# Seven pairs of 128-column blocks of an input projection, half of their rows by products of 2x2 blocks; weight sums moved from VectorE to GpSimd

## The chip, the cores and the metric

The kernel runs on one core of a Trainium2 chip. The metric is the device time of one execution in microseconds (us), as the median of three runs. Engines are named as in the profile: PE (TensorE, its weight loads apart as PEld), DVE (VectorE), ACT (ScalarE), POOL (GpSimd), SP (SyncE, here only an issuer of DMAs).

## The reference

One layer of a decoder: a norm, one input projection, three kinds of token mixers on disjoint heads, one output projection, a last norm. There are 512 tokens behind 16 meta tokens, 2048 channels, and all of it is float32.

```python
h = rms_norm(concat(meta, x), norm_w)              # 528 rows of 2048
proj = h @ w_in                                    # 2048 x 7585 columns
# 6 DeltaNet heads:  dq, dk, dv -> causal conv, SiLU, chunked delta rule, norm, * silu(dz)
# 5 GLA heads:       gq, gk, gv -> gated linear attention, norm, * silu(gz)
# 5 attention heads: logits = (fq * 128**-0.5) @ fk.T + c_t - c_s, causal softmax,
#                    o_fox = probs @ fv * silu(fz)
o = concat(o_dn, o_gla, o_fox)                     # 16 heads of 128
y = rms_norm(x + o @ w_out, final_norm_w)
```

## The kernel before

It is one program. A scheduler sets the order of the instructions on each engine from the order in the program, priorities and waits; pools of a fixed number of buffers set when a tile can be used again. There is a place where the order is written out by hand: `PLACE`, `PM` and `behind` put some matmuls of the mixers behind a given matmul of the projection, so that TensorE has projection work while other engines prepare a mixer's step.

**Arithmetic.** A float32 product is made of three passes of TensorE over operands that are split exactly into two parts, high and low: high by high, high by low, low by high. The norm's weight is worked into the transposed input when it is loaded, and its 16 tiles of 128 channels (k-tiles) stay in SBUF as `xh` and `xl`, 528 columns each. A weight tile is loaded by SP into `raw` (128x1024), its high part is made by ScalarE (L150), its low part by VectorE (L151), at the highest priority (`split`). The pool `wp` holds two each of `raw`, `hi` and `lo`.

**Input projection.** `inproj(key)` makes a block of 128 output columns for all tokens: two weight tiles of 8 k-tiles, each k-tile with three passes (`inproj_part`, L207). With the meta tokens a pass is two matmuls of 264 columns, which go to two PSUM banks; without them it is one of 512. The pool `psb` has four such banks, `psm` four more for all else. `evac` (L325) then multiplies with 1/rms of each token (`rstd`) on VectorE.

**Order of the work.** Four dz blocks while x is loaded; the gates; DeltaNet in two groups of three heads, each `dn_keys`, `dn_values`, `dn_queries`, `dn_inverse`, `dn_mix`; the gz gates; GLA in three pairs of heads; five attention heads; the output projection; the norm. `conv_silu` makes DeltaNet's keys, values and queries: `evac`, four VectorE instructions of convolution (L418), then `silu`, whose first step is on GpSimd (L334), three on ScalarE and the last on VectorE (L338). Behind it TensorE transposes keys (L490, tile `pk`) and values (L628, tile `pv`).

**Attention.** `fox_head(h)` makes the blocks fk and fv (with meta tokens), fq and fz (without), and then four blocks of 128 queries with softmax. The gated output stays in a tile of the pool `zp` (or a `gd` or `six` tile).

**Output projection.** The heads are ordered 6 DeltaNet, 5 GLA, 5 attention. The last eight go through plain products (`mms`, L1068). The first eight (`SH`) are taken in pairs of heads, as 2x2 blocks, by seven products in place of eight (Winograd's form). This needs sums of weight blocks: `weight_sums(j, half)` loads four 128x512 blocks of `w_dn`, makes four subtractions on VectorE (L432) in a tile of `six` and stores them to DRAM (`tw`). Eight calls of it stand in attention heads 0 to 3 (`SUMS`). The sums of the operands begin in `first_sums` (VectorE, attention head 4). The final weight is applied by GpSimd (L1092).

The output's accumulators and the gated heads share `zp`, 11 tiles of 128x512.

## Time and profile before

| | |
|---|---|
| median of three runs | 1009.97 us (1009.96, 1009.97, 1011.5) |
| the profiled execution | 1010.53 us |
| its span in the trace | 1008.8 us |
| granted TensorE clock, mean | 0.998 |
| moved by DMA | 128.13 MB, mean 127 GB/s |
| idle time of TensorE in the span | 1008.8 - 995.7 = 13.1 us |

The span reaches from the first to the last instruction in the trace; the run takes 1.7 us more. The profile gives busy times of each engine, the chain of waits that ended last, groups of instructions by line and tile with the wait before them, and the engines' pieces in time. A row of a group reads: line, engine, operation, output and inputs with their shape, count; busy time and mean duration; idle time just before, and what ended it.

### The profile page before, as it was taken

How to read it: one execution, taken by the hardware profiler on the slowest of the kernel's cores; microseconds unless marked ns; L12 is line 12 of the kernel's file. 1: busy time of each engine (PE TensorE's matmuls, PEld its weight loads, DVE VectorE, ACT ScalarE, POOL GpSimd, SP SyncE). 2: the span in 40 equal slices, each digit the busy share in tenths (PEclk: the TensorE clock that was granted, in tenths of full speed). 3: DMA queues.
4: the chain of work that ended last, by engine and by line, in shares of the span. 5: the costliest groups of instructions: out<-in, count | busy, mean ns of one | idle time of the engine just before them, and what ended most of it. 6: DMA issues, size and time to landing. Idle time of an engine off the chain costs nothing.

```text
span 1008.8 us, 19003 instructions
## 1 busy us (share of the span) xinstructions
PE 995.7 (99%) x7614; PEld 898.7 (89%) x7614; DVE 618.2 (61%) x1342; ACT 433.1 (43%) x948; POOL 138.6 (14%) x141
## 2 busy tenths in 40 slices
PE   9999999999999999999999999999999999999996
PEld 7899999899999888898989988889898988888885
DVE  6366767865566985244646474655363747677673
ACT  7654533434456334244445444342323244354354
POOL 0021411211112322101111010100101010000060
PEclk9999999999999999999999999999999999999999
DMA  9623233233222223231221272543362635466634
GB/s 351 229 67 119 82 93 96 102 101 104 75 86 75 94 90 101 68 94 59 84 64 50 66 244 82 189 138 93 120 226 95 237 119 188 127 193 226 181 109 167
DMA packets 53357, 128.13 MB, mean 127 GB/s; under 512 B 11949, under 2 KB 15197, under 8 KB 53268
## 3 DMA queue, kind: packets, MB, share of 16 engines
q1 hardware_dynamic: 39008, 115.30, 34.5%
q10 hardware_dynamic: 14260, 11.61, 4.1%
q8 instruction: 60, 0.98, 0.4%
q14 instruction: 29, 0.24, 0.1%
HBM read 113.32 MB, written 13.44 MB: 126 GB/s over the span
## 4 chain that ended last, share of the span: by engine, by line
PE 92%; DVE 3%; ACT 1%; DMA 1%; POOL 1%; issue 1%; ACTq 1%; SPq 0%; DVEq 0%; POOLq 0%
PE pp L207 57%; PE pa L1068 5%; PE pq L1068 4%; PE pp L261 4%; PE pt L1068 4%; PE ps L1068 2%; PE pss L822 1%; PE pr L1068 1%; POOL stgz L334 1%; PE pgate L361 1%; PE pfo L990 1%; PE pfa L957 1%; DVE wlo L151 1%; DVE ot L556 1%; PE pg L523 1%
## 5 line engine op out<-in xcount | busy, mean ns | idle before, releaser
L207 PE MATMUL pp<-xl,whi 128*128 128x264 f32 (+2 forms) x1456 | 378.1, 310 | 0.0
L207 PE MATMUL pp<-xh,whi 128*128 128x264 f32 (+2 forms) x1456 | 376.3, 310 | 0.8 <-DVE fqk L325 0.7
L207 PE MATMUL pp<-xh,wlo 128*128 128x264 f32 (+2 forms) x1456 | 375.4, 309 | 0.4 <-DVE wlo L151 0.4
L207 PEld LDWEIGHTS pp<-xh,whi 128*128 128x128 f32 x1456 | 243.1, 188 | 15.1 <-issue 1.4
L207 PEld LDWEIGHTS pp<-xl,whi 128*128 128x128 f32 x1456 | 244.3, 189 | 13.6 <-issue 0.2
L207 PEld LDWEIGHTS pp<-xh,wlo 128*128 128x128 f32 x1456 | 243.7, 188 | 14.1 <-DVE wlo L151 0.8
L150 ACT CAST whi<-raw 128x1024 fp32r<-128x1024 f32 x110 | 115.3, 1048 | 184.7 <-PE pp L207 158.1
L151 DVE TENSOR_TENSOR wlo<-raw,whi 128x1024 fp32r<-128x1024 f32 x110 | 134.4, 1222 | 88.8 <-ACT whi L150 78.2
L334 POOL TENSOR_SCALAR stc<-cv 128x528 f32<-128x528 f32 (+1 forms) x18 | 28.2, 1566 | 138.2 <-DVE cv L418 115.2
L418 DVE SCALAR_TENSOR_TENSOR cv<-pb,cpk,cv 128x528 f32<-128x528 f32 (+1 forms) x54 | 40.7, 755 | 0.7
L1068 PE MATMUL pa<-whio,ol 128*128 128x512 f32 x72 | 28.5, 396 | 0.0
L1068 PE MATMUL pa<-wloo,oh 128*128 128x512 f32 x72 | 28.3, 393 | 0.0
L325 DVE TENSOR_TENSOR pb<-pp,rstd 128x264 f32<-128x264 f32 (+1 forms) x36 | 13.7, 423 | 23.3 <-PE pp L207 23.3
L432 DVE TENSOR_TENSOR ws<-ws 128x512 f32<-128x512 f32 x32 | 21.6, 686 | 9.7 <-DMA ws<-in_w_dn 9.6
L150 ACT CAST whis<-raws 128x1024 fp32r<-128x1024 f32 x16 | 16.8, 1051 | 24.8 <-PE pq L1068 9.7
L151 DVE TENSOR_TENSOR wlos<-raws,whis 128x1024 fp32r<-128x1024 f32 x16 | 19.5, 1222 | 12.7 <-ACT whis L150 12.7
L1068 PE MATMUL pa<-whio,oh 128*128 128x512 f32 x72 | 26.6, 399 | 0.0
L977 ACT CAST fphi<-pfx 128x384 fp32r<-128x384 f32 (+2 forms) x20 | 8.0, 399 | 41.0 <-PE pfx L974 38.2
L966 ACT ACTIVATE fp<-fp,fsm 128x144 f32<-128x144 f32 (+3 forms) x20 | 11.5, 574 | 29.8 <-DVE fsm L965 29.7
L150 ACT CAST whio<-rawo 128x1024 fp32r<-128x1024 f32 x13 | 13.7, 1051 | 24.1 <-PE pa L1068 12.8
L334 POOL TENSOR_SCALAR stfz<-zfz 128x512 f32<-128x512 f32 x5 | 10.6, 2126 | 94.9 <-ACT whi L150 47.8
L1092 POOL TENSOR_TENSOR acc<-acc,fw 128x512 f32<-128x512 f32 x3 | 4.6, 1564 | 135.2 <-ACT sqf L1089 135.2
(439 smaller groups left out, 1642.7 us busy)
## 6 DMA issues: line engine op xcount, KB each, us to landing
raw<-in_w_in SPq DMA_DIRECT2D x110, 512.0 KB, 3.3
ws<-in_w_dn SPq DMA_DIRECT2D x32, 256.0 KB, 4.7
tw<-ws SPq DMA_DIRECT2D x32, 256.0 KB, 3.5
rawo<-in_w_out SPq DMA_DIRECT2D x13, 512.0 KB, 3.4
raws<-tw SPq DMA_DIRECT2D x12, 512.0 KB, 4.6
xt<-in_xtok SPq DMA_DIRECT2D x8, 512.0 KB, 8.7
rawa<-in_w_dn SPq DMA_DIRECT2D x8, 512.0 KB, 3.6
xs<-in_xT SPq DMA_DIRECT2D x7, 528.0 KB, 7.1
```

Of the source, the lines that this page charges most:

```text
L150: pace[0] = A.copy(hi, raw).ins
L151: pace[1] = V.tensor_tensor(out=lo, in0=raw, in1=hi.bitcast(F32), op=ALU.subtract).ins
L207: mm = PE.matmul(p_[:, :nt], wt[:, j * m : (j + 1) * m], xx[k][:, t0 : t0 + nt], start=(k == 0 and wt is hi and xx is xh), stop=(k == KT - ...
L261: mm = PE.matmul(ps[:, :S], wt[:, j * P : (j + 1) * P], xx[k][:, NM:T], start=(k == 0 and wt is hi and xx is xh), stop=(k == KT - 1 and wt ...
L325: V.tensor_tensor(out=o, in0=p_[rows], in1=rstd[rows, t0 : t0 + n], op=ALU.mult)
L334: G.tensor_scalar_max(t, src, LOW)
L361: PE.matmul(pgate[a][:, :HT], wg[k // 8][:, k % 8, :], xx[k][:, a * HT : (a + 1) * HT], start=(k == 0 and xx is xh), stop=(k == KT - 1 and ...
L418: V.scalar_tensor_tensor(out=c, in0=pb[:, t0 + w : w + T], scalar=cwc[:, blk, w : w + 1], in1=c, op0=ALU.mult, op1=ALU.add)
L432: sub = lambda o, a, b: V.tensor_tensor(out=o, in0=a, in1=b, op=ALU.subtract)
L523: PE.matmul(pg[:r, j * r : (j + 1) * r], kT[:, j, ts], kT[:, j, ts], start=True, stop=True)
L966: A.activation(pr[:, : m + P], pr[:, : m + P], AF.Exp, bias=sm[:, 2:3], accum_out=sm[:, 3:4])
L1068: PE.matmul(p_, o_[:, s], w_, start=(first and n == 0), stop=(last and n == 2), skip_group_check=True)
```

## The change

Three things change together.

**Pairs of blocks.** In attention heads 1 to 4 the four blocks are taken as two pairs, (fk, fq) and (fv, fz); the first of them, (fk, fq) of head 1, is left as it was, so seven pairs remain. `inproj_pair` makes both blocks of a pair. Of the 16 k-tiles, 0 to 3 and 8 to 11 form a product of 2x2 blocks: two blocks of columns by two halves of channels, times two halves of channels by two halves of tokens (264 each, `lo_` with the meta tokens and `hi_`). It is made as seven products of blocks; the other eight k-tiles are added plainly. All of it runs in four PSUM banks (a, b, c, d), in 15 calls of `mm` with 12 matmuls each. Four blocks of summed weights come from DRAM (`ti`), made ahead by `in_sums` on GpSimd. The sums of x are made by `x_sums` (GpSimd, with splits on ScalarE and VectorE), and the last by `x_last`, which overwrites the second half of `xh` and `xl` of k-tiles 0 to 3 in head 1.

**Weight sums.** `weight_sums` runs on GpSimd too, with its staging in `zp` in place of `six`. Its eight calls and the seven of `in_sums` stand between the steps of DeltaNet (`AHEAD`): in the first group behind `dn_keys` three `in_sums`, behind `dn_values` three, behind `dn_queries` one, behind `dn_inverse` two `weight_sums`; the other six in the second group.

**Room.** Gated DeltaNet heads and the first two GLA heads are stored to DRAM (`zd`) and loaded again ahead of the output projection, so that their tiles are free for staging and for `x_sums`. `zp` has 12 tiles of 128x528. `first_sums` runs on GpSimd, as a step of the output projection.

```diff
+NK = 4
+H1 = 1
+SKIP = 1
+LATE = 1
+ZK = 3
...
-    zp = pool("zp", 11)
+    zp = pool("zp", 12)
...
+    def in_sums(n):
+        h, one, two = PAIRS[n]
+        x, y, z = stage(f"is{n}")
+        get = lambda o, key, half: nc.sync.dma_start(out=o, in_=w_in[BLOCK_OF[key, h], half][:, :KC])
+        put = lambda i, t: nc.sync.dma_start(out=ti[n][:, i], in_=t)
+        two_ = lambda o, a, b, op: G.tensor_tensor(out=o, in0=a, in1=b, op=op)
+        get(x, two, 0)
+        get(y, two, 1)
+        get(z, one, 0)
+        two_(y, x, y, ALU.add)
+        two_(x, z, x, ALU.subtract)
+        put(0, y)
+        two_(z, y, z, ALU.subtract)
+        put(2, x)
+        put(1, z)
+        get(x, one, 1)
+        two_(x, x, z, ALU.subtract)
+        put(3, x)
...
+    def x_sums(ks):
+        for k in ks:
...
+            two = lambda o, p_, q_, op=ALU.subtract: G.tensor_tensor(out=o, in0=p_, in1=q_, op=op)
+            two(a, B(0, 0, 1), B(0, 0, 0))
+            two(b, B(1, 0, 1), B(1, 0, 0))
+            two(a, a, b, ALU.add)
+            parts("t1", 0, a)
+            two(b, B(0, 1, 1), a)
+            two(b, b, B(1, 1, 1), ALU.add)
+            parts("t2", 1, b)
+            two(a, B(0, 1, 0), b)
+            two(a, a, B(1, 1, 0), ALU.add)
+            parts("t4", 2, a)
...
+    def x_last(last):
...
+            else:
+                A.copy(xh[k][:, HT:], xr[k])
+                V.tensor_tensor(out=xl[k][:, HT:], in0=xr[k], in1=f(xh[k]), op=ALU.subtract)
+
+    def inproj_pair(n, c1, c2, tmp):
...
+        w1, w2 = tile_of("1", both(b1, head_))
+        mm(a, w1, xs_(up, lo_), True, True)
+        A.copy(ta, a[:, :HT])
+        mm(b, w2, xs_(dn, lo_), True)
+        def two():
...
+            w1, w2 = tile_of("2", ti[n][:, 0:2])
+            mm(d, w1, sums("t1"), True, True)
+            A.copy(tb, d[:, :HT])
+            mm(a, w2, sums("t2"), False, True)
+            V.tensor_tensor(out=tb, in0=a[:, :HT], in1=tb, op=ALU.add)
+
+        def three():
...
+            w1, w2 = tile_of("3", both(b1, rest_))
+            mm(b, w1, xs_(r0, lo_))
+            mm(b, w2, xs_(r1, lo_), False, True)
+            V.tensor_tensor(out=c1[:, lo_], in0=b[:, :HT], in1=ta, op=ALU.add)
+            mm(c, w1, xs_(r0, hi_), True)
+            mm(c, w2, xs_(r1, hi_))
+
+        c = d = None
+        for f in (three, two) if n < LATE else (two, three):
+            f()
+        w1, w2 = tile_of("4", ti[n][:, 2:4])
+        mm(a, w1, xs_(up, hi_), False, True)
+        A.copy(ta, a[:, :HT])
+        mm(c, w2, xs_(dn, hi_), False, True)
+        V.tensor_tensor(out=c1[:, hi_], in0=c[:, :HT], in1=tb, op=ALU.add)
+        w1, w2 = tile_of("5", w_in[b2, 0][:, rest_], w_in[b2, 1][:, head_])
+        mm(d, w1, xs_(r0, hi_))
+        mm(a, w2, sums("t4"), cols=dead)
+        mm(a, w1, xs_(r0, lo_), cols=dead)
+        w1, = tile_of("6", w_in[b2, 1][:, rest_])
+        mm(d, w1, xs_(r1, hi_), False, True)
+        V.tensor_tensor(out=c2[:, hi_], in0=d[:, :HT], in1=ta, op=ALU.add)
+        mm(a, w1, xs_(r1, lo_), False, True, cols=dead)
+        A.copy(c2[:, dead], a[:, dead])
...
-        w = six.tile([P, 3, 512], F32, tag="six", name=f"ws{j}{half}")
-        x, y, z = (w[:, i] for i in range(3))
+        x, y, z = stage(f"ws{j}{half}")
...
-        sub = lambda o, a, b: V.tensor_tensor(out=o, in0=a, in1=b, op=ALU.subtract)
+        sub = lambda o, a, b: G.tensor_tensor(out=o, in0=a, in1=b, op=ALU.subtract)
...
+            if 2 * p + e < SH - DN_HEADS:
+                nc.sync.dma_start(out=zd[DN_HEADS + 2 * p + e], in_=o)
...
+            n = 2 * (h - H1) - SKIP
...
+                inproj_pair(n, kT, qT, qk[:, 1])
+                G.tensor_tensor(out=kT, in0=kT, in1=rstd, op=ALU.mult)
...
+            if h == H1:
+                x_last(True)
...
+            inproj_pair(n + 1, v, zr, qk[:, 1])
+            G.tensor_tensor(out=v, in0=v, in1=rstd, op=ALU.mult)
+            vhi, vlo, v3, vm = values(v)
+            G.tensor_tensor(out=zr[:, NM:], in0=zr[:, NM:], in1=rstd[:, NM:], op=ALU.mult)
...
-    SUMS = {h: [(h, 0), (h, 1)] for h in range(4)}
-    FS = 4
+    SUMS = {}
+    XLAST = 0
+    AHEAD = {(0,0):(0,1,2),(0,1):(3,4,5),(0,2):(6,),(0,3):((0,0),(0,1)),(1,0):((1,0),(1,1)),(1,1):((2,0),(2,1)),(1,2):((3,0),(3,1))}
+    XSUM = {1: (0,), 2: (1,2), 9:(3,)}
...
         st = dn_keys(g)
+        ahead(g, 0)
         dn_values(g, st)
+        ahead(g, 1)
         dn_queries(g, st)
+        ahead(g, 2)
         dn_inverse(g, st)
+        ahead(g, 3)
         dn_mix(g, st)
+        for h in range(H * g, H * g + H):
+            nc.sync.dma_start(out=zd[h], in_=zs["dz", h])
...
+    for i in range(SH):
+        key = ("dz", i) if i < DN_HEADS else ("gz", i - DN_HEADS)
+        zs[key] = zp.tile([P, T], F32, tag="zs", name=f"zr{i}")[:, :S]
+        nc.sync.dma_start(out=zs[key], in_=zd[i])
...
-    steps.append(lambda: rest(EARLY, EARLY + 1))
+    steps.append(lambda: (first_sums(), rest(EARLY, EARLY + 1)))
```

More of the change, by code (lines that the diff above doesn't have):

```diff
@@ L347, in gate_z @@
         if t is None:
-            t = zp.tile([P, S], F32, tag="zs", name=f"zs{kind}{h}")
+            t = zp.tile([P, T], F32, tag="zs", name=f"zs{kind}{h}")[:, :S]
         silu(t, z[:, :S], f"{kind}{h}")
@@ L915, in fox_head @@
-        v = row(f"vf{h}")[:, :T]
-        evac(inproj(("fv", h)), v)
-        pv = psm.tile([P, 512], F32, tag="m", name=f"pvf{h}")
-        for b in range(NB):
-            PE.transpose(pv[:, b * P : (b + 1) * P], v[:, bsl(b)], ident)
-        vhi, vlo = (row(f"v{n}{h}", dt=F32R)[:, :S] for n in ("hi", "lo"))
-        v3 = t15(f"v3{h}", (P, P))
-        A.copy(vhi, pv)
-        V.tensor_tensor(out=vlo, in0=pv, in1=vhi.bitcast(F32), op=ALU.subtract)
-        A.copy(v3, pv[:, 3 * P :])
-        v4 = t15(f"v4{h}", (P, 2 * NB, NM))
@@ L939, in fox_head @@
                         base=0, channel_multiplier=1, compare_op=ALU.is_ge, fill=BIG)
-        if h == FS:
-            first_sums()
+        if h + 1 < FOX_HEADS:
+            ahead_[h + 1] = six.tile([P, 3, T], F32, tag="six", name=f"fqk{h + 1}")
+            G.memset(ahead_[h + 1][:, 1, 0:1], 0.0)
+        if h == H1 - 1:
+            x_sums(XSUM.get(9, ()))
+            x_last(False)
         if h in SUMS:
@@ L1018, in tile_hybrid_trunk @@
     for p in range(3):
+        x_sums(XSUM.get(p, ()))
         gla_pair(p)
@@ L1022, in tile_hybrid_trunk @@
     for h in range(FOX_HEADS):
+        x_sums(XSUM.get(3 + h, ()))
+        if h == H1 and XLAST:
+            x_last(False)
         fox_head(h)
@@ L1055, in begin @@
     def begin(tb, cc, load=True):
-        if len(acc) < 11 - SH:
-            acc[tb, cc] = zp.tile([P, S], F32, tag="zs", name=f"acc{cc}{tb}")
+        if len(acc) < 12 - SH:
+            acc[tb, cc] = zp.tile([P, T], F32, tag="zs", name=f"acc{cc}{tb}")[:, :S]
         else:
```

131 lines of the change are left out of this document (117 added, 14 removed).

## The prediction

> **What bounds the kernel now.** Four views, in this order: the page's busy shares, the chain that ended last, the busy time of each engine in three stretches, and TensorE's pieces in time.
>
> ```profile
> span 1008.8 us, 19003 instructions
> PE 995.7 (99%) x7614; PEld 898.7 (89%) x7614; DVE 618.2 (61%) x1342; ACT 433.1 (43%) x948; POOL 138.6 (14%) x141
> PEclk9999999999999999999999999999999999999999
> PE 92%; DVE 3%; ACT 1%; DMA 1%; POOL 1%; issue 1%; ACTq 1%; SPq 0%; DVEq 0%; POOLq 0%
> ```
> ```profile
> 63.00:160.00 97.00, 97.00 (x810) 96.52 (x809) 72.09 (x164) 39.78 (x88) 19.01 (x23) 1.00 0.31 99
> 195.00:275.00 80.00, 80.00 (x806) 78.46 (x806) 48.80 (x102) 33.64 (x71) 14.66 (x16) 1.00 0.30 94
> 634.00:820.00 186.00, 185.31 (x1171) 166.82 (x1170) 100.34 (x254) 62.35 (x122) 15.17 (x16) 1.00 0.45 151
> ```
>
> The columns of the second fence are: stretch, length, then busy us of PE, PEld, DVE, ACT, POOL, the clock and the DMA engines' share. The reader is to see that TensorE is busy in every stretch, at full clock, and makes 92% of the chain. GpSimd (POOL) has much room on average (19 of 97 us in the first stretch, DeltaNet's first group), VectorE less (72 of 97). So two things count: products that go, and anything that makes TensorE wait.
>
> **The products.** What one costs is read from two long pieces of the chain in the attention heads:
>
> ```profile
> 700.11 8.35 PE pp L207 x36
> 731.04 8.35 PE pp L207 x68
> ```
>
> The first holds products of 512 columns, the second of 264: 8.35/36 = 0.2319 us and 8.35/68 = 0.1228 us apart. (The mean durations of the page, 310 ns, overlap and are not used.) Between them a column costs 0.00044 us, so one of 248 columns is 0.1158.
>
> Two blocks before: one with the meta tokens, 16 x 3 x 2 = 96 products of 264, one without, 48 of 512: 96 x 0.1228 + 48 x 0.2319 = 22.92 us. After, `inproj_pair` calls `mm` 15 times with 12 products: 12 calls of 264 and 3 of 248 columns: 144 x 0.1228 + 36 x 0.1158 = 21.85 us. That is 1.07 us a pair, and with seven pairs **-7.5 us**. It is this small because only half of the input rows go through the seven products, and 36 more instructions carry 0.007 us each. The Trainium skill ("TensorE: Matmul & The Clock Gate", "Wait — 56ns, not 53.3ns?") puts a product at columns / 2.4 GHz + 2.5 ns; by that the seven pairs would give 8.1 us (an estimate). The rows here are 10 ns (264) and 16 ns (512) above it, and I go by the rows.
>
> **What the sums cost beside DeltaNet.** Sixty additions of 128x512 go to GpSimd: 28 (`in_sums`, new) and 32 (`weight_sums`, until now on VectorE in the attention heads). In DeltaNet's first group stand 36 (seven and two sums of four), in the second 24. First the rows, of GpSimd's product with the final weight, which has the same shape, and of VectorE at that time:
>
> ```profile
> L784 POOL TENSOR_TENSOR gpr<-gqk 128x512 f32<-128x512 f32 x2 | 2.6, 1290 | 0.0
> 967.49 2.57 POOL L1092 TENSOR_TENSOR acc<-acc,fw 128x512 f32<-128x512 f32 x2 [135.02 <-ACT sqf L1089]
> 970.24 2.07 POOL L1092 TENSOR_TENSOR acc<-acc,fw 128x512 f32<-128x512 f32 x1 [0.18 <-ACT sqf L1089]
> 972.26 5.78 POOL L1092 TENSOR_TENSOR accs<-accs,fw 128x512 f32<-128x512 f32 x3
> 971.66 1.20 DVE L151 TENSOR_TENSOR wll<-rawl,wlh 128x512 fp32r<-128x512 f32 x1
> L432 DVE TENSOR_TENSOR ws<-ws 128x512 f32<-128x512 f32 x32 | 21.6, 686 | 9.7 <-DMA ws<-in_w_dn 9.6
> L843 POOL TENSOR_TENSOR gkd<-gkd,gqk 128x512 f32<-128x512 f32 x2 | 5.3, 2675 | 57.8 <-ACT gkd L842 57.8
> ```
>
> Alone an addition takes 1.29 us. Beside VectorE's splits six take 2.57 + 2.07 + 5.78 = 10.42, 1.74 each; the worst row has 2.68. VectorE suffers too: its 512-wide subtraction takes 1.20 there, 0.69 elsewhere. I take c = 1.74, the row nearest to it (same operation, VectorE dense), and keep 1.29 and 2.68. The room left is (97 - 19)/36 = 2.17 us for each, so on average it fits.
>
> In order it is tighter, as GpSimd also does the first step of each SiLU (L334, 1.53 us), whose results TensorE waits for by name:
>
> ```profile
> 101.89 1.53 POOL L334 TENSOR_SCALAR stc<-cv 128x528 f32<-128x528 f32 x1 [7.12 <-DVE cv L418]
> 106.07 0.71 DVE L338 TENSOR_TENSOR kT<-cv,stc 128x528 f32<-128x528 f32 x1 [0.67 <-ACT stc L337]
> 109.42 0.60 PE L490 MATMUL pk<-ident,kT 128*16 128x128 f32 x4
> 122.74 1.53 POOL L334 TENSOR_SCALAR stc<-cv 128x528 f32<-128x528 f32 x1
> 127.48 0.68 DVE L338 TENSOR_TENSOR v<-cv,stc 128x528 f32<-128x528 f32 x1
> 130.61 0.60 PE L628 MATMUL pv<-ident,v 128*128 128x128 f32 x4
> L526 POOL TENSOR_SCALAR_AFFINE_SELECT e<-e 128x384 f32<-128x384 f32 x4 | 4.7, 1196 | 1.2 <-ACT e L525 1.2
> L502 POOL TENSOR_SCALAR_AFFINE_SELECT at<-at 128x384 f32<-128x384 f32 x4 | 2.2, 544 | 0.6 <-DVE kd L500 0.5
> ```
>
> (The last two rows are groups of the stretch 102 to 122.8.) Slack is 109.42 - 106.78 = 2.6 us for the third head's keys and 130.61 - 128.16 = 2.4 for the first values; the changed kernel's order puts the latter's transposes 45 products later, so 2.4 + 45 x 0.1228 = 7.9. Ahead of the keys' step GpSimd's order now has 18 additions and two SiLU steps: from about 66, when the first loads have landed, to 101.89 there are 35.9 us for 18c + 3.1: 34.4 with c = 1.74, in time. From there to the values' step: 1.5 + 10c + 7.3 for the masks (4.7 + 2.2 + 0.4) = 26.2 in 20.9 us, 5.3 late, within 7.9. The next has 6 additions in 12.5 us and catches up. So nothing by c = 1.74 itself, but the margins are 1.5 to 2.6 us; I put **+1.0** for loads that land late.
>
> A wait is added on the queue of SyncE (SP) too: each store of a sum waits for GpSimd, and behind it stand the next loads of weights (`raw`), for which ScalarE, VectorE and then TensorE wait. The cover is the double buffer:
>
> ```profile
> raw<-in_w_in SPq DMA_DIRECT2D x110, 512.0 KB, 3.3
> ws<-in_w_dn SPq DMA_DIRECT2D x32, 256.0 KB, 4.7
> tw<-ws SPq DMA_DIRECT2D x32, 256.0 KB, 3.5
> L150 ACT CAST whi<-raw 128x1024 fp32r<-128x1024 f32 x110 | 115.3, 1048 | 184.7 <-PE pp L207 158.1
> L151 DVE TENSOR_TENSOR wlo<-raw,whi 128x1024 fp32r<-128x1024 f32 x110 | 134.4, 1222 | 88.8 <-ACT whi L150 78.2
> ```
>
> A tile of 1024 columns feeds 48 x 0.1228 = 5.9 us of products, two tiles 11.8. Landing 3.3 and splitting 1.05 + 1.22 leave 11.8 - 5.6 = 6.2 us by which SP may be late. Traffic: 72 transfers of 0.262 MB and 18 of 0.524 in 97 us, 292 GB/s, where the trace shows 351 in its first slice: full, not over. The second group's 24 additions have 80 us with 14.7 us of other work, and the keys of that group are ready long before; together with `x_sums` (28 short additions, in the GLA pairs and head 0) I put **+0.5**, between 0 and the first group's +1.0 twice.
>
> **The attention heads.** The 32 subtractions (21.6 us of VectorE) leave, but TensorE waits for nothing there now (185.31 of 186), so that gains nothing. Against it, a pair has six weight tiles for four, split in 11 halves: 11 x (0.69 - 1.22 x 4/11) = 2.7 us more VectorE and, with four PSUM copies, some 4 us more ScalarE a pair, both with room (100 and 62 of 186). The cover gets thin: tiles of 24 products last 24 x 0.1228 = 2.95 us, two 5.9, where the shortest was 24 x 0.2319 = 5.6.
>
> ```profile
> L150 ACT CAST wlh<-rawl 128x512 fp32r<-128x512 f32 x6 | 3.4, 619 | 3.3 <-DMA rawl<-in_w_out 3.3
> L151 DVE TENSOR_TENSOR wll<-rawl,wlh 128x512 fp32r<-128x512 f32 x6 | 5.0, 855 | 1.9 <-ACT wlh L150 1.9
> DMA to landing us min/median/max: 3.2/3.3/4.2
> ```
>
> (The last row is for `raw` in the stretch 634 to 820.) A buffer comes round in 3.3 + 0.62 + 2 x 0.69 + some 0.3 for the issue = 5.6 us, against 5.9: it holds, with 0.3 us to spare, and the next tile of 48 products gives 2.95 back. With a landing of 4.2 or a split behind other work it does not. Bounds: nothing, and 1 us in each pair (7); I take 0.3 a pair, **+2.0**, nearer to the row that holds. The evacuations inside a pair (0.4 us each) lie under the products of the other three banks; the in-place change of `xh` (`x_last`) lies behind the pair's third tile.
>
> The saved heads' way to memory and back (16 transfers of 256 KB) and `first_sums` on GpSimd lie under the 86 us of the output projection's first 9 steps: nothing.
>
> **Sum.** -7.5 + 1.0 + 0.5 + 2.0 = **-4.0 us**. The profiled execution took 1010.53 us, its span 1008.8; the median of the three runs is 1009.97, so **1006.0**.
>
> **Rivals.**
> 1. GpSimd late beside VectorE. For: 2.68 us above, and splits and convolutions that read two operands of SBUF are much of VectorE's 72 us. Against: 1.74 in the densest row. With a backlog from the start the values' step is 28c - 44.9 us late, less 7.9 of slack: free up to c = 1.89, and the whole 7.5 is gone at c = 2.15. At 2.2, between 1.74 and 2.68, TensorE waits 8.8 us: 1009.97 - 7.5 + 8.8 + 2.5 = **1014**, slower. The Trainium skill ("SBUF — State Buffer", "Who interferes with whom") says that a VectorE instruction with two SBUF inputs and a GpSimd one that reads SBUF exclude each other for the whole instruction; the rows (2.07 for 1.29, 1.20 for 0.69) bear out that both lose, but VectorE lost 0.5 us there, not 1.29.
> 2. The short tiles do not come in time: 1 us a pair, 1009.97 - 7.5 + 7 + 1.5 = **1011**, within the bound. For: 0.3 us to spare. Against: landings are steady (3.2 to 4.2).
> 3. The products do not get cheaper as counted: before, neighbours of 264 columns go to two PSUM banks in turn; now 12 in a row go to one. No row shows that with 264; with 512 it is the rule. 7.5/(7 x 180) = 6 ns more each would eat the gain: **1010** to 1013.
>
> **Chances.** About 0.2% (2 us) is what a measurement tells from no change: faster is below 1008, slower above 1012. Forecast 0.50 (faster). Rival 1: 0.23 (slower). Rival 2: 0.19 (0.15 same, 0.04 slower). Rival 3: 0.08 (0.05 same, 0.03 slower). So 0.50, 0.20, 0.30. The range: down to no wait at all, 1002.5; up to rival 1 at c = 2.27 (28 x 0.07 = 2 us more than at 2.2), 1016.
>
> **What would show it.** In the profile after: products of 264 columns 0.123 apart within a pair (rival 3: 0.129); additions of 1.6 to 1.9 us in 63 to 160 (rival 1: over 2.1, and TensorE idle ahead of the transposes of keys or values); TensorE idle in the pairs under 0.5 us each, ended by a split (rival 2: 1 us). The forecast is wrong if TensorE's idle time grows by more than 7.5 us, wherever.

## The result, and the profile after

The changed kernel takes **1032.78 us** (median of five runs, 1030.3 to 1034.33) against 1010.0: ratio 1.0217, interval 1.02 to 1.0234, so 2.2% slower. The forecast was 1006.0, and the range ended at 1016.

The page of the changed kernel, its heads and the chain that ended last:

```profile
span 1032.5 us, 19949 instructions
PE 999.1 (97%) x7866; PEld 915.4 (89%) x7866; DVE 678.5 (66%) x1389; ACT 460.0 (45%) x1041; POOL 283.2 (27%) x252
PEclk9999999998999999999999999999999999999999
PE 73%; DVE 14%; POOL 4%; DMA 3%; ACT 3%; issue 2%; ACTq 1%; SPq 0%; DVEq 0%; POOLq 0%
```

TensorE is idle for 1032.5 - 999.1 = 33.4 us where it was 13.1, and VectorE and GpSimd have come onto the chain. The mean clock fell from 0.998 to 0.988, worth some 12.4 - 2.0 = 10.4 us. So the difference of the spans, 23.7 us, is 20.3 us of idle time, about 10.4 us of clock, and about -7 us that are left for the products: they did get cheaper.

Where it went is read from the times at which the same product of the plain input projection starts in both traces (L207 before, L212 after): the one behind the first 48, 768, 1536 and 3264, then the first product of the output projection, and the end. The fourth cut lies half-way through the first block of head 1, so the stretch that is called GLA holds head 0 as well. In us longer than before:

| kernel | start | DeltaNet, group 1 | group 2 | mix, gz, GLA | heads | output | sum |
|---|---|---|---|---|---|---|---|
| changed | 0.5 | **14.6** | **13.7** | 1.5 | **-6.9** | 0.3 | 23.7 |

The loss lies almost wholly beside DeltaNet. There TensorE waits at these places (the timeline of the changed kernel; in brackets the idle time before, and what ended it):

```profile
102.09 0.51 PE L212 MATMUL pp<-xh,wlo 128*128 128x264 f32 x2 [1.86 <-DVE wlo L156]
118.26 0.61 PE L654 MATMUL pk<-ident,kT 128*16 128x128 f32 x4 [2.13 <-DVE kT L343]
139.77 1.01 PE L687 MATMUL pg<-kT 128*128 128x128 f32 x6 [4.24 <-DVE anm L694]
231.98 0.52 PE L212 MATMUL pp<-xh,wlo 128*128 128x264 f32 x2 [4.17 <-DVE wlo L156]
250.60 1.49 PE L738 MATMUL pm<-iv,an 32*32 32x32 f32 x48 [3.62 <-DVE iv L732]
```

Together these five are 16.0 us. Each of them ends with a VectorE instruction. Is VectorE late because its inputs are, or because it is slow? The two groups, cut at the same products, before and then after (columns as in the prediction's second fence: stretch, length, PE, PEld, DVE, ACT, POOL, clock, DMA's share and GB/s):

```profile
60.80:160.90 100.10, 100.10 (x836) 99.62 (x835) 74.09 (x166) 41.96 (x93) 20.18 (x25) 1.00 0.30 96
160.90:281.30 120.40, 120.40 (x1055) 114.68 (x1054) 81.33 (x170) 51.56 (x103) 20.91 (x21) 1.00 0.30 95
```
```profile
61.30:176.00 114.70, 104.82 (x835) 102.97 (x834) 94.78 (x162) 41.67 (x93) 75.37 (x59) 0.97 0.75 245
176.00:310.20 134.20, 125.22 (x1055) 119.03 (x1054) 99.97 (x176) 51.52 (x103) 59.45 (x46) 0.96 0.55 182
```

These rows nearly close the account. TensorE was idle for 114.70 - 104.82 = 9.9 us in the first group and for 134.20 - 125.22 = 9.0 in the second, where it had been busy throughout; the clock of 0.97 and 0.96 is worth some 3.4 and 5.4 us. That is 27.7 of the 28.3 us.

And groups of instructions in the first group, from 63 to 160, before and after:

```profile
L151 DVE TENSOR_TENSOR wlo<-raw,whi 128x1024 fp32r<-128x1024 f32 x15 | 18.3, 1217 | 11.4 <-ACT whi L150 11.4
L418 DVE SCALAR_TENSOR_TENSOR cv<-pb,cpk,cv 128x528 f32<-128x528 f32 x18 | 13.6, 758 | 0.2
L325 DVE TENSOR_TENSOR pb<-pp,rstd 128x264 f32<-128x264 f32 x12 | 4.6, 424 | 8.2 <-PE pp L207 8.2
```
```profile
L156 DVE TENSOR_TENSOR wlo<-raw,whi 128x1024 fp32r<-128x1024 f32 x12 | 18.9, 1578 | 3.4 <-ACT whi L155 3.4
L581 DVE SCALAR_TENSOR_TENSOR cv<-pb,cpk,cv 128x528 f32<-128x528 f32 x15 | 17.3, 1153 | 0.2
L330 DVE TENSOR_TENSOR pb<-pp,rstd 128x264 f32<-128x264 f32 x10 | 3.8, 421 | 0.0
L429 POOL TENSOR_TENSOR is<-is,is 128x512 f32<-128x512 f32 x28 | 44.1, 1592 | 8.2 <-DMA is<-in_w_in 7.7
L594 POOL TENSOR_TENSOR ws<-ws,ws 128x512 f32<-128x512 f32 x7 | 9.9, 1415 | 3.0 <-DMA ws<-in_w_dn 2.8
```

For the same products of TensorE VectorE was busy 20.7 us longer in the first group (74.09 to 94.78) and 18.6 in the second (81.33 to 99.97): 0.65 us for each of the 60 additions that GpSimd made. The convolution's step went from 758 to 1153 ns, the split from 1217 to 1578. The evacuation, whose first operand lies in PSUM, stayed at 421 for 424. GpSimd's additions took 1.59 and 1.42 us, less than the 1.74 of the forecast.

How an instruction is held shows best in a run of short ones on the changed kernel's timeline, at the end of a series of additions:

```profile
219.19 8.04 POOL L594 TENSOR_TENSOR ws<-ws,ws 128x512 f32<-128x512 f32 x6 [4.61 <-DMA ws<-in_w_dn]
222.10 1.30 DVE L722 TENSOR_TENSOR ab<-ab,ot 51x150 f32<-51x150 f32 x1
226.04 1.31 DVE L720 TENSOR_TENSOR ot<-ab 51x108 f32<-51x108 f32 x1
227.39 0.26 DVE L722 TENSOR_TENSOR ab<-ab,ot 51x108 f32<-51x108 f32 x1
```

The additions end at 227.23. Until then each VectorE instruction takes 1.3 us, as long as one addition; the next of the same shape takes 0.26. The Trainium skill ("SBUF — State Buffer", "Who interferes with whom") states that a VectorE instruction with two inputs in SBUF contends with a GpSimd instruction that reads SBUF, for an exclusive lock, and that one with at most one input in SBUF, outside certain modes, does not. The rows above agree, the evacuation with its operand in PSUM (421 for 424) too. The prediction had set that reading aside.

In the heads TensorE waited for two things only (the waits of TensorE, 660 to 860: us, times, longest), and twelve products of 264 columns in a row on one bank take 1.47 us (a piece of the chain of waits):

```profile
PE pp_b L516 <- DVE wlo L156: 1.1, 1, 1.1
PE pp_a L516 <- ACT fqk L558: 1.0, 1, 1.0
```
```profile
752.23 1.47 PE pp_a L516 x12
```

### The profile page after: what moved, and what is told of

Read it like the earlier page. It is cut to its first block, busy times and chain, and to the rows that moved or that the text cites. A ratio compares the mean times of both kernels' runs of the same rounds, so it can differ in the third digit from the quotient of the medians.

```text
span 1032.5 us, 19949 instructions
## 1 busy us (share of the span) xinstructions
PE 999.1 (97%) x7866; PEld 915.4 (89%) x7866; DVE 678.5 (66%) x1389; ACT 460.0 (45%) x1041; POOL 283.2 (27%) x252
## 3 DMA queue, kind: packets, MB, share of 16 engines
q8 instruction: 62, 1.02, 0.4%
## 4 chain that ended last, share of the span: by engine, by line
PE 73%; DVE 14%; POOL 4%; DMA 3%; ACT 3%; issue 2%; ACTq 1%; SPq 0%; DVEq 0%; POOLq 0%
PE pp L212 25%; PE pp_a L516 6%; PE pa L1291 5%; PE pp L266 4%; PE pq L1291 4%; PE pt L1291 4%; PE pp_d L516 3%; DVE wlo L156 3%; PE pp_c L516 3%; PE pp_b L516 3%; PE ps L1291 2%; DVE cv L581 2%; POOL is L429 1%; DVE ab L722 1%; DVE ot L720 1%
## 5 line engine op out<-in xcount | busy, mean ns | idle before, releaser
L212 PE MATMUL pp<-xh,wlo 128*128 128x264 f32 (+2 forms) x1120 | 286.3, 309 | 6.3 <-DVE wlo L156 6.3
L212 PE MATMUL pp<-xh,whi 128*128 128x264 f32 (+2 forms) x1120 | 286.2, 309 | 2.0 <-ACT whi L155 1.2
L212 PE MATMUL pp<-xl,whi 128*128 128x264 f32 (+2 forms) x1120 | 286.1, 308 | 0.0
L156 DVE TENSOR_TENSOR wlo<-raw,whi 128x1024 fp32r<-128x1024 f32 (+1 forms) x159 | 157.9, 1008 | 97.8 <-ACT whi L155 91.7
L212 PEld LDWEIGHTS pp<-xh,wlo 128*128 128x128 f32 x1120 | 189.5, 192 | 16.5 <-DVE wlo L156 7.4
L155 ACT CAST whi<-raw 128x1024 fp32r<-128x1024 f32 (+1 forms) x159 | 129.8, 838 | 163.1 <-PE pp L212 85.3
L212 PEld LDWEIGHTS pp<-xh,whi 128*128 128x128 f32 x1120 | 189.6, 191 | 11.8 <-ACT whi L155 1.4
L212 PEld LDWEIGHTS pp<-xl,whi 128*128 128x128 f32 x1120 | 189.7, 191 | 8.5
L594 POOL TENSOR_TENSOR ws<-ws,ws 128x512 f32<-128x512 f32 x32 | 45.3, 1429 | 23.1 <-DMA ws<-in_w_dn 19.5
L429 POOL TENSOR_TENSOR is<-is,is 128x512 f32<-128x512 f32 x28 | 44.1, 1592 | 8.2 <-DMA is<-in_w_in 7.7
L516 PE MATMUL pp_a<-xl,whi 128*128 128x264 f32 (+1 forms) x112 | 27.7, 281 | 0.0
```

Of the source, the lines that this page charges most:

```text
L155: pace[0] = A.copy(hi, raw).ins
L156: pace[1] = V.tensor_tensor(out=lo, in0=raw, in1=hi.bitcast(F32), op=ALU.subtract).ins
L212: mm = PE.matmul(p_[:, :nt], wt[:, j * m : (j + 1) * m], xx[k][:, t0 : t0 + nt], start=(k == 0 and wt is hi and xx is xh), stop=(k == KT - ...
L429: two_ = lambda o, a, b, op: G.tensor_tensor(out=o, in0=a, in1=b, op=op)
L516: m = PE.matmul(p_[:, cols], wt[:, j * P : (j + 1) * P], xx[j][part_][:, cols], start=first and i == 0, stop=last and i == len(todo) - 1, ...
L594: sub = lambda o, a, b: G.tensor_tensor(out=o, in0=a, in1=b, op=ALU.subtract)
```

## The experiments

**Theory P (ports):** GpSimd's additions hold VectorE's instructions, whose chains then come late for TensorE; the clock halves after the longer waits. **Theory Q (queue and traffic):** the sums' 120 transfers and SP's waiting stores make the weights late. **Rival 1 of the prediction:** GpSimd itself is late for the first step of SiLU. The numbers of all runs of the trunk, in the table's terms (us longer than before; in the last column median and, with an interval, the ratio; what each run changes is said below):

| kernel | group 1 | group 2 | mix to GLA | heads | output | time |
|---|---|---|---|---|---|---|
| e1_no_adds | 0.6 | 4.1 | 1.4 | -6.9 | 0.2 | 1010.12 |
| e2_adds_only | 18.6 | 12.2 | -1.4 | -6.8 | 0.1 | 1033.85 |
| e3_quarters | 26.3 | 16.2 | -1.1 | -6.7 | 0.3 | 1045.58 |
| e5_ws_heads | 13.7 | 0.0 | 0.1 | -5.4 | 38.2 | 1057.28 |
| e6_v_gz | 0.0 | 0.0 | 10.5 | -4.6 | 38.0 | 1052.47, 1.0418 (1.0398 to 1.0438) |
| e7_g_gz | 0.0 | -0.1 | 14.5 | -4.7 | 38.2 | 1058.02, 1.0486 (1.0444 to 1.0528) |
| e8_v_same | 4.6 | -1.3 | 15.3 | -6.9 | 0.2 | 1023.21 |
| e9_v_gla | 0.0 | 0.0 | 16.5 | 13.8 | 0.3 | 1041.27, 1.03 (1.0277 to 1.0324) |
| e10_g_gla | 0.0 | 0.0 | 22.1 | 16.1 | 0.2 | 1046.0, 1.0357 (1.0335 to 1.038) |
| e11_pairs_alone | 0.0 | -0.1 | -1.6 | -6.7 | 0.2 | 1004.22, 0.9938 (0.992 to 0.9956) |
| e12_memsets | 8.8 | 9.2 | 0.0 | -6.8 | 0.4 | 1022.29 |
| e13_silu_vector | 21.9 | 12.1 | 0.5 | -7.7 | 0.8 | 1038.25 |
| e14_v_first | 2.0 | -0.1 | 2.1 | 11.9 | 0.4 | 1024.94, 1.0142 (1.0121 to 1.0164) |
| e15_ws_only | 0.0 | -0.1 | 1.0 | 12.0 | 0.4 | 1023.43, 1.0118 (1.0095 to 1.0142) |
| e16_v_spread | 2.4 | 1.1 | -1.5 | 11.1 | 0.4 | 1025.38, 1.0165 (1.0138 to 1.0191) |
| e17_v_late | 7.6 | 1.5 | 2.3 | -1.4 | 2.9 | 1021.8, 1.0116 (1.0095 to 1.0137) |
| e18_v_late3 | 2.4 | 0.0 | 0.7 | 0.2 | 4.9 | 1019.27, 1.0096 (1.008 to 1.0111) |

(The stages are of the profiled execution. The GLA column moves by some 1.5 us either way with a wait of TensorE on its own queue, "issue", which was 1.32 us before, 1.8 in the changed kernel, and absent in e2 and e11. Times without an interval are single runs; beside them the kernel before had medians from 1009.6 to 1011.3.)

**Additions or transfers (e1, e2).** e1 takes the additions out of `in_sums` and `weight_sums` (`two_` and `sub` do nothing) and keeps loads and stores; e2 keeps the additions, on operands taken from the resident x, and takes loads and stores out.

```diff
-        two_ = lambda o, a, b, op: G.tensor_tensor(out=o, in0=a, in1=b, op=op)
+        two_ = lambda o, a, b, op: None
...
-        sub = lambda o, a, b: G.tensor_tensor(out=o, in0=a, in1=b, op=ALU.subtract)
+        sub = lambda o, a, b: None
```
```diff
-        get = lambda o, key, half: nc.sync.dma_start(out=o, in_=w_in[BLOCK_OF[key, h], half][:, :KC])
-        put = lambda i, t: nc.sync.dma_start(out=ti[n][:, i], in_=t)
+        get = put = lambda *a: None
...
-            w1, w2 = tile_of("2", ti[n][:, 0:2])
+            w1, w2 = tile_of("2", both(b1, head_))
```

> The 60 additions of the weight sums on GpSimd are left out; all loads and stores of them stay (the loaded blocks themselves are stored, so the output is not the reference's). In the changed kernel the DeltaNet stage came out 28 us longer than before, the GLA stage 1.7 us, the heads' stage 7 us shorter. Theory P (ports): GpSimd's additions hold up VectorE's instructions, whose chains then end last. Expects DeltaNet's excess under 4 us and a total of 1005 to 1009 us. Theory Q (queue and traffic): 120 more transfers fill the DMA engines and SP's stores hold back the weights' loads. Expects an excess of 15 us or more to stay, total over 1018, with weights landing in 4.5 us or more and TensorE waiting for splits whose loads came late.

> The other half: the 60 additions stay on GpSimd at their places (their operands are taken from the resident x), their loads and stores are left out, and the products read plain weights in place of the sums, so the output is not the reference's. Theory P: most of the 28 us stay, since nothing that holds VectorE is gone: DeltaNet's excess 15 to 28 us, total 1018 to 1032. Theory Q: excess under 4 us, total 1003 to 1008.

The windows of the two groups, e1 first, then e2:

```profile
61.00:161.60 100.60, 100.42 (x835) 99.55 (x835) 74.48 (x166) 41.96 (x93) 19.25 (x25) 1.00 0.82 284
161.60:286.10 124.50, 121.97 (x1055) 116.09 (x1054) 82.24 (x170) 52.01 (x103) 21.30 (x21) 0.99 0.59 193
```
```profile
61.40:180.10 118.70, 104.98 (x836) 103.55 (x835) 102.73 (x167) 43.49 (x97) 85.22 (x61) 0.94 0.25 81
180.10:312.70 132.60, 125.19 (x1055) 118.73 (x1054) 99.54 (x170) 49.87 (x100) 57.33 (x44) 0.96 0.28 86
```

With all transfers and no additions VectorE's busy time is that of before (74.48, 82.24), though the DMA engines move 284 GB/s in the first group; with additions and no transfers it is 102.73 and 99.54. P holds for most of it: 30.8 us in the two groups from additions alone, 4.7 from transfers alone. Together that is 35.5, more than the changed kernel's 28.3, so the two do not simply add; and e2 lost more than P expected (15 to 28 us, a total of 1032 at most). In e1 the stores wait for loads alone and not for GpSimd; but e2, which has no store at all, loses as much, so that wait is not needed for the loss. Q's part is not nothing: the 4.1 us of e1's second group begin with a wait of 2.53 us for `iv` at 227.53, a round trip through memory by DMA. The last of the five waits above, 3.62 us for `iv`, goes back to the same place: on the chain the store of `ab` to memory took 9.15 us there and 10.36 in e1, but 5.25 in e2. So that wait is in part the transfers'. The total of e1, 1010.12 against 1011.29 of the same session, missed the 1005 to 1009 that P expected.

**The ports by themselves (e4).** A kernel without the trunk, in stretches such as these:

```python
for g, v, n, m in ((g_add, v_two, 12, 20), (g_add, v_psum, 12, 20), (g_add, v_one, 12, 20), (g_add, v_short, 12, 40),
                   (g_add, v_copy, 12, 40), (g_one, v_two, 12, 20), (g_one, v_psum, 12, 20), (g_set, v_two, 12, 20)):
```

> No trunk: only GpSimd and VectorE, each alone and then side by side, in a row of stretches (GpSimd 128x512 additions, one-operand maxima, memsets; VectorE 128x512 additions from SBUF, the same with one operand from PSUM, one-operand products, 128x12 additions, 128x128 copies). Strict form of P: an addition alone 1.29 us and VectorE's 0.69; side by side they alternate, so each takes about 1.9 to 2.0 from its predecessor's end, a 128x12 addition rises from about 0.1 to 1.3, and with one operand from PSUM neither slows. Rate sharing: a 128x12 addition stays under 0.3 and a 128x512 one rises to at most 1.0-1.2.

GpSimd's and VectorE's rows on its timeline (start, length, of so many instructions): the first three alone (GpSimd's addition, VectorE's addition, its one-operand product), then side by side with VectorE's two operands in SBUF, with one in PSUM, with one operand in all, and with twelve columns:

```profile
12.59 10.64 POOL L105 TENSOR_TENSOR go<-ot 128x512 f32<-128x512 f32 x8
42.03 5.78 DVE L114 TENSOR_TENSOR vo<-ot 128x512 f32<-128x512 f32 x8
55.08 3.66 DVE L120 TENSOR_SCALAR vo<-ot 128x512 f32<-128x512 f32 x8
64.80 20.02 POOL L105 TENSOR_TENSOR go<-ot 128x512 f32<-128x512 f32 x12
64.68 25.78 DVE L114 TENSOR_TENSOR vo<-ot 128x512 f32<-128x512 f32 x20
91.33 16.06 POOL L105 TENSOR_TENSOR go<-ot 128x512 f32<-128x512 f32 x12
91.22 14.47 DVE L117 TENSOR_TENSOR vo<-pt,ot 128x512 f32<-128x512 f32 x20
107.89 20.46 DVE L120 TENSOR_SCALAR vo<-ot 128x512 f32<-128x512 f32 x20
129.10 19.65 DVE L123 TENSOR_TENSOR vo<-ot 128x12 f32<-128x12 f32 x40
```

Alone an addition takes 1.33 us and VectorE's 0.72. Side by side they alternate: twelve of each in 20.02 us, 1.67 for a pair, so GpSimd loses a quarter and VectorE more than doubles. With an operand in PSUM both are as alone (1.34 and 0.72). VectorE's one-operand product is held too (20.46 for 20, where 9.2 would do). Twelve columns, 0.2 us each alone, take 0.63 on the mean beside additions and 1.2 at most; 25 of them ran beside the 12 additions, two for each. The two-operand forms, with and without PSUM, come out as in the rows of the changed kernel; the 1.9 to 2.0 that I expected of a pair was too much, as some 0.4 us of the two overlap.

**Smaller pieces (e3).** Each addition as four of 128 columns.

```diff
-        two_ = lambda o, a, b, op: G.tensor_tensor(out=o, in0=a, in1=b, op=op)
+        def two_(o, a, b, op):
+            for i in range(0, 512, P):
+                G.tensor_tensor(out=o[:, i : i + P], in0=a[:, i : i + P], in1=b[:, i : i + P], op=op)
```

> The same sums, each addition as four of 128 columns, one after the other. If VectorE waits for a whole GpSimd instruction (P in its strict form), its short instructions beside them fall from 1.2-1.3 us to about 0.5, their chains get shorter and DeltaNet's excess falls from 28 to some 10-20 us: total 1013 to 1025. If the two only share the port's rate, or if loads and the queue are the cause (Q), no change or a little more for the starts of 240 instructions in place of 60: 1030 to 1038.

```profile
L431 POOL TENSOR_TENSOR is<-is,is 128x128 f32<-128x128 f32 x112 | 60.2, 572 | 12.0 <-DMA is<-in_w_in 12.0
L343 DVE TENSOR_TENSOR kT<-cv,stc 128x528 f32<-128x528 f32 x3 | 7.4, 2458 | 18.9 <-ACT stc L342 18.9
```

A miss: 1045.58, which neither theory had expected. A quarter takes 572 ns, four of them 2.29 us for 1.59, probably because each may wait for a VectorE instruction. So here GpSimd is late as well: SiLU's first step for the first and the third keys began 7.6 and 5.5 us behind the convolution, with GpSimd busy until then, and before SiLU's last step VectorE sat idle for 18.9 us in the first group, where it was 7.6 in the changed kernel. VectorE's step itself takes 2458 ns, longer than any one piece; that several pieces hold it in turn is a reading, not shown.

**GpSimd busy without reading (e12), and SiLU off GpSimd (e13).** Both start from e2.

```diff
-        two_ = lambda o, a, b, op: G.tensor_tensor(out=o, in0=a, in1=b, op=op)
+        def two_(o, a, b, op):
+            for _ in range(3):
+                G.memset(o, 1.0)
```
```diff
-        G.tensor_scalar_max(t, src, LOW)
+        V.tensor_scalar_max(t, src, LOW)
```

> As the kernel with the additions alone (no loads, no stores, plain weights in place of the sums), but each addition is replaced by three GpSimd memsets of 128x512 (0.575 us each by the stretch of memsets measured by itself, 1.73 us together, about what an addition took beside VectorE). GpSimd's queue is as full as before and SiLU's first steps stand behind it in the same way, but it reads no SBUF. P, VectorE held up: DeltaNet's excess falls from 31 to under 5 us, total 1003 to 1009. Rival 1 as the prediction put it, GpSimd late for the SiLU steps: the excess stays, 15 us or more, total over 1018.

> The kernel with the additions alone (60 additions on GpSimd beside DeltaNet, no loads or stores, plain weights in place of the sums; total 1034, DeltaNet's excess 31 us), with the first step of each SiLU on VectorE in place of GpSimd. Rival 1 (GpSimd late for SiLU): that wait is gone, excess under 8 us, total 1003 to 1012. P (VectorE held up by the additions): the additions are still there and VectorE has one instruction more for each SiLU: excess 15 us or more, total 1018 to 1040.

By its numbers e12 falls on the side that was expected of rival 1: 18.0 us in the two groups (15 or more) and 1022.29 (over 1018). Its groups of VectorE (63 to 160) say why this decides nothing:

```profile
L582 DVE SCALAR_TENSOR_TENSOR cv<-pb,cpk,cv 128x528 f32<-128x528 f32 x18 | 13.7, 760 | 0.3
L580 DVE TENSOR_SCALAR cv<-pb,cpk 128x528 f32<-128x528 f32 x6 | 12.3, 2043 | 0.4
```

Beside memsets the two-operand step of the convolution is free (760 ns), but its one-operand step, 490 to 496 ns otherwise, takes 2043 on the mean and up to 5.8 us: memsets hold that form, and for several of them in a row. So e12 still holds VectorE up and does not part the two theories. e13 decides: with SiLU off GpSimd's queue the first group is 21.9 us longer than before, where it was 18.6 in e2, and the total is 1038.25, within P's 1018 to 1040. That SiLU stands behind the additions in GpSimd's queue is not the cause. The changed kernel's own timeline says the same: all three of SiLU's first steps for the keys found GpSimd idle, waiting for VectorE's convolution (two are shown).

```profile
84.32 2.44 POOL L339 TENSOR_SCALAR stc<-cv 128x528 f32<-128x528 f32 x1 [1.46 <-DVE cv L581]
112.67 2.43 POOL L339 TENSOR_SCALAR stc<-cv 128x528 f32<-128x528 f32 x1 [0.65 <-DVE cv L581]
```

**The additions elsewhere (e5 to e8).** e5 puts `weight_sums` back on VectorE in heads 0 to 3 and keeps `in_sums`; e6 also moves `in_sums` to VectorE among the gz gates, e7 leaves it on GpSimd there; e8 has all additions at the changed kernel's places, on VectorE.

```diff
-    SUMS = {}
+    SUMS = {h: [(h, 0), (h, 1)] for h in range(4)}
...
+        for n in ((0, 1), (2, 3), (4,), (5,), (6,))[h]:
+            in_sums(n)
...
-        sub = lambda o, a, b: G.tensor_tensor(out=o, in0=a, in1=b, op=ALU.subtract)
+        sub = lambda o, a, b: V.tensor_tensor(out=o, in0=a, in1=b, op=ALU.subtract)
```

> weight_sums goes back to VectorE in attention heads 0 to 3; in_sums stays on GpSimd beside DeltaNet's first group. Theory P: the second group has no additions left and loses its 13.8 us; the first has 28 for 35, in the same order, and keeps 10 to 13; the heads take 21.6 us more on VectorE, which has room: total 1015 to 1020 us. Rival: the weights' tiles in the heads come late once VectorE is fuller there (up to 1 us a pair): 1020 to 1027.

> No sums beside DeltaNet's first group and most of the second: in_sums on VectorE among the gz gates, weight_sums on VectorE in the heads. If P is the whole cause, only the pairs' gain of 7 us and the 1.5 to 2 us of the GLA stage are left: 1003 to 1006 us, faster than before by 0.4 to 0.7%. Rival: VectorE in the heads becomes the bound with 32 subtractions on top of the pairs' eleven splits: 1007 to 1013.

> As the kernel with the sums among the gz gates, but the 28 additions of in_sums on GpSimd there. If what counts is that VectorE is on the path beside them (P), it costs little where VectorE is busy 45 of 100 us: within 3 us of the version on VectorE, 1003 to 1009. If GpSimd's additions cost by themselves wherever they stand, it loses 28/60 of 28 us, 13 us more than the version on VectorE: 1015 to 1019.

> All 60 additions at the changed kernel's places beside DeltaNet, but on VectorE (0.69 us each). VectorE has 72 of 97 us of work in the first group; 36 additions make 25 more, 97 of 97: it is then the bound there, but nothing holds it up and GpSimd is free for SiLU. P expects DeltaNet's excess between the 4 us without additions and the 28 with GpSimd: 8 to 20 us, total 1012 to 1026. If the port is not the cause, the work moved onto the busier engine makes it worse than 1033.

e5 bears P out where it can be read: no additions in the second group, nothing lost there; 28 in the first, 13.7 lost (10 to 13 expected). The totals of e5, e6 and e7 all missed what was expected (at most 1027, 1013 and 1019), for another reason. The reload of the saved heads (`zr`, SP's rows of the timeline) in the changed kernel and in e6, and a window of e6:

```profile
831.08 0.80 SPq L1255 DMA_DIRECT2D zr<-zd  x2
```
```profile
864.66 0.42 SPq L1257 DMA_DIRECT2D zr<-zd  x1
```
```profile
880.00:890.00 10.00, 0.00 (x0) 0.00 (x0) 2.19 (x6) 2.33 (x7) 2.22 (x4) 0.50 1.02 359
```

In the heads `zp` is full: nine tiles of `x_sums` and three gated heads. So `weight_sums`, staged there, could not start before the pairs were done (in e6 its subtractions run from 817.2 to 891.0), held the reload up until 864.66 (831.08 in the changed kernel, although e6 reaches the output projection earlier, at 834.3 for 851.7), and collided with it and the accumulators' loads. TensorE stands still from 880 to 890 with the DMA engines full. My edits had made a new wait; these 38 us say nothing on the change. e6 and e7 also show that `in_sums` by the gz gates costs 10 to 15 us, on either engine. e8 loses 4.6 us in the first group, a third of the loss with GpSimd, though VectorE does 36 additions more. Its second group has another order of products, so that -1.3 and 15.3 are to be read together: 14 us, no better than with GpSimd.

**Does any place keep the pairs' gain (e11, e9, e10, e14 to e18)?** e11 leaves all work for the sums out.

> The pairs without any work for the sums: no additions, loads or stores of in_sums and weight_sums; the products read plain weight blocks in place of the sums, so the output is not the reference's. It prices what the products gain by themselves, with the six short weight tiles of a pair. P and the trace of the changed kernel (heads 7 us shorter, GLA 1.5 to 2 longer, output projection +0.5): 1003 to 1006 us. If the gain in the heads hangs on VectorE being rid of weight_sums there and no more, or on the late start, 1007 or more.

1004.22, 6.1 us faster (ratio 0.9938): that is what the products are worth with their short tiles, with `x_sums` and the saved heads' way left in. e9 and e10 stage both kinds of sums in `six`, put `weight_sums` on VectorE in heads 0 to 3 and spread `in_sums` over GLA and two heads (e9 VectorE, e10 GpSimd; `INS` below); e14 has `in_sums` on VectorE in DeltaNet's first group (`AHEAD` below), e16 spreads it thinner; e15 has `weight_sums` in the heads alone.

```diff
+    INS = {0: (0, 1), 1: (2, 3), 2: (4,), 3: (5,), 4: (6,)}
...
-    AHEAD = {(0,0):(0,1,2),(0,1):(3,4,5),(0,2):(6,),(0,3):((0,0),(0,1)),(1,0):((1,0),(1,1)),(1,1):((2,0),(2,1)),(1,2):((3,0),(3,1))}
+    AHEAD = {(0,0):(0,1,2),(0,1):(3,4,5),(0,2):(6,)}
...
+        w = six.tile([P, 3, 512], F32, tag="six", name=f"ws{j}{half}")
+        x, y, z = (w[:, i] for i in range(3))
```

> All sums on VectorE, none beside DeltaNet: in_sums spread over the three GLA pairs and heads 0 and 1 (two, two, one, one, one calls), weight_sums in heads 0 to 3, the staging in tiles of the pool six and no longer in zp, where it had held back the heads' reload and the accumulators (output projection 38 us longer in the two kernels before). Expects DeltaNet's excess under 0.5 us, GLA's 1 to 2, the heads' gain of 7 us kept within 1.5 and the output projection as in the changed kernel (+0.5): total 1003 to 1006 us. Rival: the transfers in GLA and in the heads make the short weight tiles late, 0.5 us or more for each pair and transfer of a call: 1008 to 1013.

> The same, but the 28 additions of in_sums on GpSimd in the GLA pairs and heads 0 and 1. By the port's rule VectorE's chains in GLA (two operands in SBUF) are held up there too, by up to an addition each: 2 to 6 us slower than the version on VectorE, 1006 to 1011. If only a dense VectorE suffers, the two are within 1.5 us.

> A version that computes the reference: in_sums at the changed kernel's places in DeltaNet's first group, on VectorE; weight_sums on VectorE in heads 0 to 3 with the staging in six, as before the change. 28 additions are 19 us of VectorE, which has 72 of 97 there; the kernel with 36 of them lost 5.5 us in that group. So 3 to 6 us there, the pairs' -6, and nothing in the heads if they have the room: 1007 to 1010, no difference or 0.3% faster. If weight_sums no longer fit into the heads beside the pairs: 1012 to 1025.

> The pairs with weight_sums on VectorE in heads 0 to 3 (staging in six), and no work for in_sums at all (plain weight blocks in place of their sums, so the output is not the reference's). If the heads have room for 32 subtractions of 0.69 us beside the pairs: 1003 to 1006, as the pairs alone (1004.2). If the double buffer, thinner with the pairs, makes the heads bound by VectorE: 1010 to 1022, with TensorE idle in the heads ahead of splits and softmax transposes.

> As the version with in_sums on VectorE in the first group, but spread thinner: two calls behind the keys, two behind the values, one behind the queries, one behind the inverse, one in the second group. If density is what costs, 2 us less than that version: 1005 to 1008; if each addition has its price wherever it stands in DeltaNet, the same within 1.5 us.

`in_sums` on VectorE beside DeltaNet's first group costs 2.0 us (e14; 3 to 6 expected) for 28 additions, where 28 on GpSimd cost 13.7 (e5). So at that place the engine counted; spreading them thinner (e16) gained nothing. The rest went wrong: in the GLA pairs and head 0 they cost 16.5 and 22.1 (e9 and e10, where 1 to 2 and a few more were expected), and in the heads `weight_sums`, which had cost nothing before the change, costs 12.0 + 6.7 = 18.7 us beside the pairs (e15). VectorE's waits in e9 (440 to 660, and 660 to 860), and e15's windows by the first pair:

```profile
DVE is L430 <- DMA is<-in_w_in: 11.8, 7, 4.5
DVE ws L595 <- DMA ws<-in_w_dn: 13.2, 11, 2.7
```
```profile
660.00:670.00 10.00, 7.09 (x38) 6.64 (x38) 5.88 (x21) 2.11 (x5) 0.73 (x2) 0.75 0.85 245
670.00:680.00 10.00, 7.43 (x35) 6.20 (x35) 4.03 (x17) 2.83 (x7) 1.33 (x1) 0.57 0.39 121
```

A sum on VectorE waits for its loads, and what stands behind it waits too (splits, softmax); as I read it, the pairs' thin double buffer passes that on to TensorE, and the clock drops (0.75 and 0.57 above). By the products' times 15 of e15's 18.7 us lie by the first pair, in heads 0 and 1. Either the place or the calls themselves could be behind that; e17 and e18 test it by moving `weight_sums` to heads 2, 3 and 4 (e18 below; e17 leaves two calls at the end of DeltaNet's first group).

```diff
-    SUMS = {}
+    SUMS = {2: [(0, 0), (0, 1), (1, 0)], 3: [(1, 1), (2, 0), (2, 1)], 4: [(3, 0), (3, 1)]}
```

> A version that computes the reference: in_sums on VectorE in DeltaNet's first group (2 us there), weight_sums on VectorE in heads 2, 3 and 4 (two calls each), the first two calls at the end of DeltaNet's first group. If the loss of weight_sums in the heads lies at the first pair, where x_last and the first weight tiles stand: -6 for the pairs, +2 to 4 in DeltaNet, +1 to 3 in the heads: 1005 to 1010 us. If it goes with the calls wherever they are: 15 us again, 1018 to 1025.

> As the version before, but all of weight_sums in the heads: three calls in head 2, three in head 3, two in head 4, none in DeltaNet. By the first reading 1005 to 1010; three calls in a head bring 1 us more each than two by their transfers (24 in some 45 us). By the second 1018 to 1025.

That it is the place holds for the heads, not for the total, which missed the 1005 to 1010 of that reading in both. e18 gives up 6.9 us of the pairs' gain there in place of 18.7, but pays 4.9 in the output projection, and 1019.27 is still 1% slower than before. No version with all sums beat the kernel before. What each place costs beyond that was not followed further.

## Why the prediction was wrong, point by point

- **The products, -7.5.** Right. Twelve products took 1.47 us, 0.1225 each, against 0.1228; rival 3 (one bank) is out. The heads came out 6.9 us shorter, the pairs alone 6.1 us in all.
- **The short weight tiles, +2.0.** Somewhat too careful: TensorE waited 2.1 us from 660 to 860, in two places, where it had waited 0.7 (185.31 of 186), and the heads came out 6.9 us shorter, where the sum had 5.5. Rival 2 is out, as long as VectorE does nothing else there (e15).
- **The sums beside DeltaNet, +1.0 and +0.5.** This step failed: 14.6 and 13.7. The duration of an addition was even a little under the forecast (1.59 and 1.42 for c = 1.74). GpSimd was late once, by 4.1 us ahead of the first values (138.66; 5.3 had been worked out), and TensorE did not wait for them, as worked out. But the step asked only when GpSimd ends. Its own rows said that VectorE loses as well (1.20 for 0.69), and no term was made of it: 60 additions at 0.5 are 30 us of VectorE, and 39 were measured, in a stage where VectorE's convolutions, masks and splits follow on one another and TensorE waits for them by name. The room was looked up as an average (72 of 97), not along that chain.
- **Rival 1** had the right side and the wrong mechanism. It priced GpSimd's lateness from c = 1.89 on; c was under that, and e13 shows that SiLU behind GpSimd's additions is not the cause. Its slower outcome came from VectorE held up, at more than its highest price.
- **SP's stores and the traffic, within the +1.0 and +0.5.** Right for the first group (0.6 in e1), too small for the second (4.1).
- **"The 32 subtractions leave ... so that gains nothing."** Right of the kernel before. With the pairs in the heads it is not: put back there, they cost 18.7 us (e15). The move and the pairs hang together.
- **Saved heads and `first_sums`, nothing.** Right (0.2), but by a margin that e5 to e7 used up.

Not settled by a run: how much of the two groups' 28.3 us would come back if one single wait were gone, how much of the second group's loss is the slow round trip of `ab`, and why `in_sums` on VectorE is cheap beside DeltaNet's first group and dear in GLA, beyond the waits for loads shown.

## What to carry to other kernels

Work given to an idle GpSimd was paid by VectorE here: price it as what it takes from VectorE's instructions with operands in SBUF, each up to a whole GpSimd instruction, along the chain that the busiest engine waits for, not against VectorE's average room. Before adding work for a gain of 0.7%, price the bare gain by leaving the work out (here 6 us), and then each place of the work by itself: a place that cost nothing before need not be free beside the change. A stage's staging tiles count as well: a pool that is full there moves the work elsewhere.

## What the hardware showed that I had not expected

**The clock after short idle times.** The granted clock (the third column from the end) falls to half after TensorE's longer waits, for 3.4 us, and for 6.8 behind the wait before 250.60. Here after the 4.24 us before 139.77:

```profile
138.00:140.00 2.00, 0.23 (x2) 0.23 (x3) 2.00 (x8) 0.00 (x0) 2.00 (x2) 1.00 0.75 188
140.00:142.00 2.00, 2.00 (x13) 2.00 (x13) 2.00 (x5) 0.65 (x1) 1.92 (x3) 0.63 0.90 291
142.00:144.00 2.00, 2.00 (x11) 2.00 (x11) 2.00 (x7) 0.00 (x0) 2.00 (x2) 0.52 0.52 168
104.00:106.00 2.00, 2.00 (x11) 2.00 (x11) 1.89 (x4) 0.00 (x0) 2.00 (x2) 0.50 0.83 305
```

The last row is behind a wait of only 1.86 us (102.09), while the 2.13 us before 118.26 had no such effect. The Trainium skill ("TensorE: Matmul & The Clock Gate", "Why this matters for your kernels") advises against gaps over some 3 us; here 1.9 us was enough once. So such a wait costs some 1.7 us more than itself, half of 3.4, and the one before 250.60 some 3.

**Memsets.** GpSimd's memsets left VectorE's two-operand instructions alone (760 ns for 758 in e12; in e4 twenty additions of 128x512 took 14.49 us beside them, 0.72 each as alone) and held one-operand ones, 2043 ns on the mean for 490 (e12).
